# Second gate/up: the last product's sum behind the split of the third quarter's rest, and both FFNs' row factor behind the down product

## The chip, the core and the metric

The kernel runs on one core of a Trainium2 chip. The metric is the device time of one execution in microseconds; lower is better.

## What is computed

One encoder layer on x of 256 rows and 2048 columns, all in float32, with F = 5632:

```python
def rms_norm(x, gain):
    return x * rsqrt(mean(x * x, axis=-1) + EPS) * gain

def swiglu(h, w_gate, w_up, w_down):
    return (silu(h @ w_gate) * (h @ w_up)) @ w_down

x = x + 0.5 * swiglu(rms_norm(x, ffn1_norm), ffn1_w_gate, ffn1_w_up, ffn1_w_down)
x = x + concat(rms_norm(s5(u)), rms_norm(attention(q, k, v))) @ w_out    # [u|q|k|v] = rms_norm(x) @ w_in
x = x + 0.5 * swiglu(rms_norm(x, ffn2_norm), ffn2_w_gate, ffn2_w_up, ffn2_w_down)
x = x + rms_norm((p @ w_ple_proj) * sigmoid(rms_norm(x) @ w_ple_gate))
```

The factor rsqrt(...) of rms_norm is one number for each row. A product of rms_norm(x) with weights is therefore computed as the product of (x times gain) with them, and the row factor r is multiplied in later.

## The kernel before

**Tiles.** T = 256 rows make two row tiles of 128 (TT = 2). F is cut into 11 column blocks of 512 (NF = 11, NB = 512), and the contraction over 2048 into four quarters of four 128-row pieces. Weights arrive by SP's DMAs as `raw` tiles, from a pool with five buffers.

**Precision.** A float32 operand is split into a high and a low part. `split` does so for two 128-row pieces at once (a half of a quarter, 128x1024): a CAST on ACT (L181) makes the high part, and a subtraction on DVE (L184) the low one. A half of a quarter and one row tile then take six matmuls on PE: high by high, low by high and high by low, twice. The results of splits lie in two rings, `whi`/`wlo` and `shi`/`slo`, which `weight_pair` hands out in turn.

**The FFNs.** In FFN1 most blocks go through the class `Seven`, which computes a 2 by 2 block product by seven products of sums. FFN2's gate and up use `Wide` for blocks f = 1 to 10. In blocks f = 1 to 9 half of the third quarter goes into the seven products too (`narrow`, the flag `n`), and the other half of that quarter, its rest, is added as an ordinary product: for the gate's columns as the first work of `column(0)`, for the up columns as the first of `column(1)`.

**`Wide.seven`.** Its products gather in the banks b2, b3, b4, b5 and b8. b3 and b8 lie in one `aux` tile, the others are `acc` tiles. The last product but one ends in b4. Then follow, in the code of before: `add(t, b21)`, two DVE additions of 128x1024 (L721) that make the operand of the last product, called "11"; `handed(b8, b4)`, an ACT copy with its sign turned (L704); the split of both sides' rests; the first half of the gate's column; the split of the sum; and product "11", which is added to b4. b4 takes no new matmul before `handed` has read it.

**The order of the work.** The program is written in one order, and a scheduler sets each engine's queue from it ahead of the run. Some instructions are kept in program order (`pin`), and `tc.issue_after` makes an instruction follow another. Each engine works through its own queue in order and waits for the others by semaphores.

**The row factor.** The norm object `xn` holds r as a tile with one column for each row tile; `xn.rs(t)` is its column t. It is used as the scale of the gate's silu (L860, L890, L925) and as the scalar of the last multiplication, up times r times gate (L870 in FFN2's `Wide` blocks, L910 in FFN1's `Seven` blocks, L950 in the others). Behind the down product `gather` (L967) adds 0.5 times a bank into x, 40 times in the two FFNs.

Of the kernel before, what the change touches and what calls it, by code (L numbers as in the profile page):

```python
# [9 lines left out]
F32 = mybir.dt.float32  # L10
# [3 lines left out]
ALU = mybir.AluOpType  # L14
AX = mybir.AxisListType

P = 128
# [9 lines left out]
NB = 512  # L27
# [6 lines left out]
def layer_kernel(ctx: ExitStack, tc: tile.TileContext, a: dict, shapes: dict, out: bass.AP):  # L34
    nc = tc.nc
# [8 lines left out]
    TT = T // P  # L44
# [7 lines left out]
    cpool = ctx.enter_context(tc.tile_pool(name="const", bufs=1))  # L52
# [46 lines left out]
    def step():  # L99
        for g in list(beside):  # L100
            if next(g, beside) is beside:
                beside.remove(g)
# [38 lines left out]
    def place_x():  # L141
        for t in range(TT):
            x = wp.tile([P, ND, NB], F32, tag="raw", name=uid("x"), bufs=5)
            xt[t][:] = [x[:, n, :] for n in range(ND)]
# [5 lines left out]
                nc.gpsimd.dma_start(xt[t][n], rows[t * P : (t + 1) * P, n * NB : (n + 1) * NB])  # L150

    place_x()
    scr_x = dramp.tile([T, D], F32, name="scr_x")

    def load_x(n):
# [482 lines left out]
    class Wide:  # L638
# [67 lines left out]
        def seven(self):  # L706

            if ring[0] is None:
                ring[:] = [self.turns, 0]
            n = self.narrow is not None  # L710
            b11 = self.load(0, 0)
            if n:
                gn, un = self.load_both(0)
                tn = self.narrow[1].tile([P, 2, NB], F32, tag="sumn", name=uid("sumn"))
            b12 = self.load(1, 0)
            b22, b21 = self.load(1, 1), self.load(0, 1)
            t = [self.pool.tile([P, 2, NB], F32, tag="sum", name=uid("sum"), bufs=2) for _ in range(2)]

            def add(x, y):
                for o, u, v in zip(t, x, y):  # L720
                    nc.vector.tensor_tensor(out=o, in0=u, in1=v, op=ALU.add)  # L721

            def add_one(o, x, y):
                nc.vector.tensor_tensor(out=tn[:, o], in0=x, in1=y, op=ALU.add)

            b2, b5 = acc(), acc()
            p = self.prepare(b11)
            self.product(b2, self.left("00"), p, True, not n)
            if n:
                pg, = self.prepare([gn])  # L730
                self.one(b2, "00", pg, 0)
            step()
            add(b11, b12)
            for u, v in zip(b12, b22):
                nc.gpsimd.dma_start(u, v, accum_op=ALU.add)
            if n:
                add_one(0, gn[:, 0], un[:, 0])
                nc.gpsimd.dma_start(un[:, 0], un[:, 1], accum_op=ALU.add)
                add_one(1, tn[:, 0], un[:, 1])
            p = self.prepare(t)  # L740
            double = aux()
            b3, b8 = double[:, :NB], double[:, NB:]
            self.handed(b3, b2)
            self.product(b5, self.left(0), p, True, not n)
            if n:
                self.one(b2, "10", pg, 1)
                pt, = self.prepare([tn])
                self.one(b5, 0, pt, 0)
            step()
            add(t, b22)  # L750
            p = self.prepare(t)
            self.product(b3, self.left(1), p)
            if n:
                self.one(b3, 1, pt, 1)
                add_one(0, tn[:, 1], gn[:, 1])
            step()
            p = self.prepare(b21)
            self.product(b2, self.left("10"), p)
            step()
            b4 = acc()  # L760
            p = self.prepare(b22)
            self.handed(b4, b3)
            self.product(b3, self.left(3), p)
            step()
            p = self.prepare(b12)
            self.product(b4, self.left(2), p)
            if n:
                pu, = self.prepare([un])
                self.one(b4, 2, pu, 0)
                self.one(b3, 3, pu, 1)  # L770
            step()
            add(t, b21)
            self.handed(b8, b4)
            self.banks = ((b2, b4), (b3, b8))
            self.double, self.five = double, b5
            self.rest = [[], []]
            if n:
                self.rest = [[(self.act(2), (1, *list(weight_split(u, 2))[0][1:]), False)] for u in self.load_both(1)]
            self.first = self.halves_of(0)
            self.half(0, *next(self.first))  # L780
            p = self.prepare(t)
            self.product(b4, self.left("11"), p)
            if n:
                pt, = self.prepare([tn[:, :1]])
                self.one(b4, "11", pt, 0)
            step()

        def halves_of(self, side):

            w, n0 = self.ws[side]  # L790
            yield from self.rest[side]
            for kb in (3,) if self.narrow else (2, 3):
                part = self.act(kb)
                for half in list(weight_halves(w, 4 * kb, 4, n0)):
                    yield part, half, kb == 3 and half[0] == 1
# [11 lines left out]
    def ffn(i, xn, nxt, bg=None):  # L807
# [30 lines left out]
        for f in range(NF):  # L838
# [9 lines left out]
            if not bg and f:  # L848
                joined = f in range(1, NF - 1)
                s = Wide(  # L850
                    xn, sums, ((wg, f * NB), (wu, f * NB)), sevens, turns, (third, narrow) if joined else None
                )
                s.seven()
                sg, hh, five = com("sg"), com("h"), com("sq")
                put_off(0, nc.scalar.copy, five, s.five)
                s.column(0)

                def gate(s=s, sg=sg):
                    for t in range(TT):
                        nc.scalar.activation(sg[:, t * NB : (t + 1) * NB], s.banks[0][t], AF.Silu, scale=xn.rs(t))  # L860

                put_off(0, gate)
                s.column(1)
                nc.vector.tensor_tensor(
                    out=hh.rearrange("p (t n) -> p t n", t=TT), in0=s.double.rearrange("p (t n) -> p t n", t=TT),
                    in1=five.unsqueeze(1).to_broadcast([P, TT, NB]), op=ALU.add,
                )
                for t in range(TT):
                    cols = slice(t * NB, (t + 1) * NB)
                    nc.vector.scalar_tensor_tensor(  # L870
                        out=hh[:, cols], in0=hh[:, cols], scalar=xn.rs(t), in1=sg[:, cols], op0=ALU.mult, op1=ALU.mult
                    )
                if f == NF - 2:
                    side.close()
                    hp = pools.enter_context(phase(f"h{i}b"))
                put_off(2, turned, hp, f, hh)
                continue
            if bg and (f >= early or f in alone):
# [25 lines left out]
                    put_off(0, opened, s)  # L904
                put_off(0, gated, s)

                def ended(s, g=gate_cols, u=up_cols, hh=hh, f=f, hp=hp):
                    nc.vector.tensor_tensor(out=hh, in0=s.banks[3.8], in1=hh, op=ALU.add)
                    for t in range(TT):
                        nc.vector.scalar_tensor_tensor(  # L910
                            out=u[t], in0=u[t], scalar=xn.rs(t), in1=g[t], op0=ALU.mult, op1=ALU.mult
                        )
                    put_off(2, turned, hp, f, hh)

                s.column(1, (1, 2, 3) if f in alone else (2, 3), True)
# [31 lines left out]
                start(prep)  # L947
            hh = com("h")
            for t in range(TT):
                nc.vector.scalar_tensor_tensor(  # L950
                    out=hh[:, t * NB : (t + 1) * NB], in0=pu[t], scalar=xn.rs(t),
                    in1=sg[:, t * NB : (t + 1) * NB], op0=ALU.mult, op1=ALU.mult,
                )
            put_off(2, turned, hp, f, hh)

        fetch_x(a["x"][0] if bg else scr_x)
# [6 lines left out]
            split(in_32(hi), in_32(lo), rows(k))  # L963
            return hi, lo

        def gather(x, ps, scale):
            nc.vector.scalar_tensor_tensor(out=x, in0=ps, scalar=scale, in1=x, op0=ALU.mult, op1=ALU.add)  # L967

        def opened(s, n):
            sg = com("sg")  # L970
            one, six = sg[:, :NB], sg[:, NB:]
            nc.scalar.copy(one, s.bank(1))
            nc.vector.tensor_tensor(out=six, in0=s.bank(6), in1=one, op=ALU.add)
            gather(xt[0][n], one, 0.5)
            for t in range(TT):
                gather(xt[t][n + 1], s.bank(5), 0.5)
            gather(xt[0][n + 1], six, -0.5)
            nc.vector.tensor_tensor(out=one, in0=s.bank(7), in1=six, op=ALU.add)
            gather(xt[1][n], one, 0.5)
            gather(xt[1][n + 1], one, -0.5)  # L980

        plans = (
            (("c", 3), ("c", 4), ("s", 0), ("c", 5), ("c", 6), ("s", 1), ("c", 7), ("c", 8), ("s", 2), ("c", 9), ("c", 10)),
# [18 lines left out]
        for n in range(0, ND, 2):  # L1002

            def end(side):
                m = n + side
                for t, z in enumerate(((2, 4), (3, 8))[side]):
                    gather(xt[t][m], s.bank(z), 0.5)
                put_off(0 if m == ND - 2 or m == ND - 1 and m < nxt.early else 2, nxt.block, m)

            s = Seven(kept, summed, ((wd, n * NB), (wd, (n + 1) * NB)), sevens, turns)  # L1010
# [1018 lines left out]
```

## Time and profile before

| what | value |
| --- | --- |
| median of 3 runs (lowest to highest) | 1821.94 us (1821.84 to 1822.03) |
| the profiled execution's own time | 1821.02 us |
| its span, first to last instruction | 1819.2 us |
| mean granted TensorE clock | 0.999 |

Time between the span and the execution's own time lies around the span. The engines are called PE (TensorE's matmuls), PEld (its weight loads), DVE (VectorE), ACT (ScalarE), POOL (GpSimd) and SP (SyncE, whose queue issues DMAs). In the timeline a row is start, duration, engine, line, operation, what it writes and reads, and in brackets how long the engine had been idle and what ended that. In a list of waits, a row is who waited for whom: total us, times, longest.

### The profile page before, as it was taken

How to read it: one execution, taken by the hardware profiler on the slowest of the kernel's cores; microseconds unless marked ns; L12 is line 12 of the kernel's file. 1: busy time of each engine (PE TensorE's matmuls, PEld its weight loads, DVE VectorE, ACT ScalarE, POOL GpSimd, SP SyncE). 2: the span in 40 equal slices, each digit the busy share in tenths (PEclk: the TensorE clock that was granted, in tenths of full speed). 3: DMA queues.
4: the chain of work that ended last, by engine and by line, in shares of the span. 5: the costliest groups of instructions: out<-in, count | busy, mean ns of one | idle time of the engine just before them, and what ended most of it. 6: DMA issues, size and time to landing. Idle time of an engine off the chain costs nothing.

```text
span 1819.2 us, 24321 instructions
## 1 busy us (share of the span) xinstructions
PE 1804.9 (99%) x8897; PEld 1491.7 (82%) x8897; DVE 1560.5 (86%) x1824; ACT 1094.0 (60%) x1285; POOL 166.1 (9%) x266
## 2 busy tenths in 40 slices
PE   9999999999999999999999999999999999999998
PEld 7888888888888888888898888788878788888887
DVE  8978889999998896697567889999999988889775
ACT  7445455656565665456695566666667656566564
POOL 0020100000000001110021002020202230000000
PEclk9999999999999999999999999999999999999999
DMA  8799867687776667674646678888877776666563
GB/s 320 268 293 300 264 224 232 233 260 228 261 262 224 187 227 250 203 252 161 218 144 223 215 267 258 278 263 253 252 229 237 256 255 240 223 206 229 192 244 127
DMA packets 106792, 430.25 MB, mean 236 GB/s; under 512 B 24784, under 2 KB 42608, under 8 KB 66576
## 3 DMA queue, kind: packets, MB, share of 16 engines
q1 hardware_dynamic: 91168, 384.28, 59.9%
q0 software_dynamic: 14784, 43.01, 10.8%
q8 instruction: 69, 1.13, 0.3%
q10 hardware_dynamic: 720, 1.41, 0.2%
q14 instruction: 51, 0.42, 0.1%
HBM read 372.41 MB, written 10.88 MB: 211 GB/s over the span
## 4 chain that ended last, share of the span: by engine, by line
PE 93%; DVE 3%; issue 1%; ACT 1%; SPq 1%; DMA 1%; DVEq 0%; ACTq 0%
PE acc L325 16%; PE acc L328 15%; PE acc L334 15%; PE aux L325 7%; PE aux L334 7%; PE aux L328 7%; PE acc L687 3%; PE acc L691 3%; PE acc L695 3%; PE acc L512 2%; PE acc L515 2%; PE acc L513 2%; PE aux L515 2%; PE aux L512 2%; PE aux L513 2%
## 5 line engine op out<-in xcount | busy, mean ns | idle before, releaser
L184 DVE TENSOR_TENSOR wlo<-raw,whi 128x1024 fp32r<-128x1024 f32 x484 | 585.9, 1224 | 128.8 <-ACT whi L181 128.2
L181 ACT CAST whi<-raw 128x1024 fp32r<-128x1024 f32 x484 | 503.4, 1050 | 316.0 <-PE acc L328 188.4
L325 PE MATMUL acc<-whi,nhi 128*128 128x512 f32 x884 | 347.4, 393 | 5.0 <-ACT whi L277 2.5
L328 PE MATMUL acc<-whi,nlo 128*128 128x512 f32 x884 | 344.4, 390 | 0.0
L334 PE MATMUL acc<-wlo,nhi 128*128 128x512 f32 x884 | 245.0, 389 | 0.0
L184 DVE TENSOR_TENSOR slo<-raw,shi 128x1024 fp32r<-128x1024 f32 x182 | 221.4, 1218 | 15.9 <-ACT shi L181 15.5
L181 ACT CAST shi<-raw 128x1024 fp32r<-128x1024 f32 x182 | 190.3, 1049 | 68.8 <-PE acc L328 21.5
L325 PEld LDWEIGHTS acc<-whi,nhi 128*128 128x128 f32 x884 | 165.9, 188 | 43.4 <-ACT whi L277 3.5
L334 PEld LDWEIGHTS acc<-wlo,nhi 128*128 128x128 f32 x884 | 165.8, 188 | 34.8 <-DVE wlo L184 0.2
L328 PEld LDWEIGHTS acc<-whi,nlo 128*128 128x128 f32 x884 | 166.0, 188 | 33.5 <-DVE nlo L278 0.2
L181 ACT CAST whi<-sum 128x1024 fp32r<-128x1024 f32 x81 | 85.2, 1053 | 123.4 <-DVE sum L519 63.2
L184 DVE TENSOR_TENSOR wlo<-sum,whi 128x1024 fp32r<-128x1024 f32 x81 | 98.4, 1220 | 8.0 <-ACT whi L181 7.9
L181 ACT CAST shi<-sum 128x1024 fp32r<-128x1024 f32 x54 | 56.8, 1052 | 77.3 <-DVE sum L519 46.3
L325 PE MATMUL aux<-whi,nhi 128*128 128x512 f32 x216 | 84.0, 389 | 0.0
L328 PE MATMUL aux<-whi,nlo 128*128 128x512 f32 x216 | 84.0, 389 | 0.0
L580 POOL DMA_DIRECT2D raw<-raw x23 | 20.1, 875 | 602.3 <-DVE sum L519 355.3
L325 PE MATMUL aux<-whi,hhi 128*128 128x512 f32 x176 | 68.5, 389 | 0.0
L328 PE MATMUL aux<-whi,hlo 128*128 128x512 f32 x176 | 68.5, 389 | 0.0
L184 DVE TENSOR_TENSOR slo<-sum,shi 128x1024 fp32r<-128x1024 f32 x54 | 65.9, 1220 | 2.8 <-ACT shi L181 2.6
L334 PE MATMUL aux<-wlo,nhi 128*128 128x512 f32 x216 | 65.2, 389 | 0.0
L519 DVE TENSOR_TENSOR sum<-sum,raw 128x1024 f32<-128x1024 f32 x50 | 61.1, 1222 | 0.8
L230 POOL DMA_DIRECT2D hT<-mid x96 | 51.6, 553 | 97.2 <-DVE mid L217 36.6
(477 smaller groups left out, 3580.9 us busy)
## 6 DMA issues: line engine op xcount, KB each, us to landing
raw<-in_ffn_w_down SPq DMA_DIRECT2D x88, 1024.0 KB, 4.9
raw<-in_ffn_w_up SPq DMA_DIRECT2D x79, 1024.0 KB, 7.2
raw<-in_ffn_w_gate SPq DMA_DIRECT2D x77, 1024.0 KB, 6.8
raw<-in_w_in SPq DMA_DIRECT2D x32, 1024.0 KB, 5.3
raw<-raw POOLq DMA_DIRECT2D x45, 512.0 KB, 7.7
raw<-in_w_out SPq DMA_DIRECT2D x16, 1024.0 KB, 5.1
raw<-in_w_ple_gate SPq DMA_DIRECT2D x16, 1024.0 KB, 5.1
raw<-in_ffn_w_gate SPq DMA_DIRECT2D x21, 512.0 KB, 7.5
```

The costliest lines, as they stand in the source:

```text
L181: copy = nc.scalar.copy(hi, src)
L184: rest = nc.vector.tensor_tensor(out=lo, in0=src, in1=hi.bitcast(F32), op=ALU.subtract)
L325: nc.tensor.matmul(ps[t], lhsT=lh, rhs=hi[:, j, cols], start=start and j == 0, stop=False, skip_group_check=joined)
L328: nc.tensor.matmul(ps[t], lhsT=ll, rhs=hi[:, j, cols], start=False, stop=False, skip_group_check=joined)
L334: nc.tensor.matmul(ps[t], lhsT=lh, rhs=lo[:, j, cols], start=False, stop=stop and j == 1, skip_group_check=joined)
L512: nc.tensor.matmul(ps, lhsT=lh[j], rhs=hi[:, j], start=begin and j == 0, stop=False)
L513: nc.tensor.matmul(ps, lhsT=ll[j], rhs=hi[:, j], start=False, stop=False)
L515: nc.tensor.matmul(ps, lhsT=lh[j], rhs=lo[:, j], start=False, stop=z in final and j == 1)
L519: nc.vector.tensor_tensor(out=t, in0=x, in1=y, op=ALU.add)
L687: nc.tensor.matmul(ps, lhsT=lh[n * i + j], rhs=hi[:, j], start=fresh and i == 0 and j == 0, stop=False, skip_group_check=True,)
L691: nc.tensor.matmul(ps, lhsT=ll[n * i + j], rhs=hi[:, j], start=False, stop=False, skip_group_check=True)
L695: nc.tensor.matmul(ps, lhsT=lh[n * i + j], rhs=lo[:, j], start=False, stop=last and i == len(parts) - 1 and j == n - 1, skip_group_check=True,
```

## The change

Two edits, made together.

1. In `Wide.seven`, for blocks with `narrow`, the split of the gate's rest is written ahead of the last product's sum. `add(t, b21)` is forced behind the DVE instruction of that split (`self.last`), and it now stands behind the fetch of the first half of the gate's column. The up side's rest is split after product "11" in place of ahead of it. `rest_of` is new.
2. In both FFNs, h is no longer multiplied by r. The two DVE instructions per block, 128x512 with a row scalar each, become one multiplication of 128x1024 by the gate (at L950 two of 128x512). `gather` multiplies by r instead: a small tile `by_row` holds 0.5 r and -0.5 r, made by two small DVE instructions ahead of each down product, and `gather` reads its scalar from there in place of the constant 0.5 or -0.5. The gate's silu keeps its r.

```diff
+    by_row = cpool.tile([P, 2 * TT], F32, name="by_row")
...
             step()
-            add(t, b21)
             self.handed(b8, b4)
...
-            self.rest = [[], []]
+            self.rest = []
             if n:
-                self.rest = [[(self.act(2), (1, *list(weight_split(u, 2))[0][1:]), False)] for u in self.load_both(1)]
+                raws = self.load_both(1)
+                self.rest.append(self.rest_of(raws[0]))
             self.first = self.halves_of(0)
-            self.half(0, *next(self.first))
+            half = next(self.first)
+            with tc.issue_after(self.last) if n else ExitStack():
+                add(t, b21)
+            self.half(0, *half)
             p = self.prepare(t)
             self.product(b4, self.left("11"), p)
             if n:
                 pt, = self.prepare([tn[:, :1]])
                 self.one(b4, "11", pt, 0)
+                self.rest.append(self.rest_of(raws[1]))
             step()

+        def rest_of(self, raw):
+            hi, lo = weight_pair()
+            self.last = split(hi, lo, raw)[1]
+            return self.act(2), (1, hi, lo), False
...
-                for t in range(TT):
-                    cols = slice(t * NB, (t + 1) * NB)
-                    nc.vector.scalar_tensor_tensor(
-                        out=hh[:, cols], in0=hh[:, cols], scalar=xn.rs(t), in1=sg[:, cols], op0=ALU.mult, op1=ALU.mult
-                    )
+                nc.vector.tensor_tensor(out=hh, in0=hh, in1=sg, op=ALU.mult)
...
-        def gather(x, ps, scale):
-            nc.vector.scalar_tensor_tensor(out=x, in0=ps, scalar=scale, in1=x, op0=ALU.mult, op1=ALU.add)
+        for sign in range(2):
+            nc.vector.tensor_scalar(
+                by_row[:, TT * sign : TT * sign + TT], xn.r[:, :TT], 0.5 - sign, None, op0=ALU.mult
+            )
+
+        def gather(t, n, ps, sign=0):
+            nc.vector.scalar_tensor_tensor(
+                out=xt[t][n], in0=ps, scalar=by_row[:, TT * sign + t : TT * sign + t + 1], in1=xt[t][n],
+                op0=ALU.mult, op1=ALU.add,
+            )
```

The line numbers of the changed kernel are higher by one up to the first edit (L181 is L182 there, L704 is L705, L721 is L722), and by more behind it. Tiles carry numbers that differ between the two kernels.

ACT's queue in block f = 3 before, from the earlier `handed` (b3 to b4) to the one that copies b4 to b8. raw_10281 is the piece with both rests, sum_10107 and sum_10108 are the halves of the last sum, sumn_10100 is the narrow block's sum, and raw_10334 the next weights:

```order
L704 ACTIVATE acc_10226<-aux_10153 128x512
L181 CAST whi_10284<-raw_10281 128x1024
L181 CAST shi_10288<-raw_10281 128x1024
L181 CAST whi_10304<-sum_10107 128x1024
L181 CAST whi_10324<-sumn_10100 128x512
L181 CAST shi_10308<-sum_10108 128x1024
L181 CAST shi_10336<-raw_10334 128x1024
L181 CAST whi_10340<-raw_10334 128x1024
L704 ACTIVATE aux_10153<-acc_10226 128x512
```

And with the change, without that first row (raw_10273 has the rests, raw_10328 the next weights):

```order
L182 CAST whi_10276<-raw_10273 128x1024
L182 CAST shi_10294<-sum_10101 128x1024
L182 CAST shi_10314<-sumn_10094 128x512
L182 CAST whi_10298<-sum_10102 128x1024
L182 CAST whi_10321<-raw_10273 128x1024
L705 ACTIVATE aux_10147<-acc_10220 128x512
L182 CAST shi_10330<-raw_10328 128x1024
L182 CAST whi_10334<-raw_10328 128x1024
```

The CAST of the up side's rest has gone from ahead of the sums' casts to behind them, and `handed` stands ahead of the next weights' two casts and still behind the sums'. DVE's queue at the same place before, from the last sum on:

```order
L721 TENSOR_TENSOR sum_10107<-sum_10107,raw_10105 128x1024
L721 TENSOR_TENSOR sum_10108<-sum_10108,raw_10105 128x1024
L184 TENSOR_TENSOR wlo_10285<-raw_10281,whi_10284 128x1024
L184 TENSOR_TENSOR slo_10289<-raw_10281,shi_10288 128x1024
L184 TENSOR_TENSOR wlo_10305<-sum_10107,whi_10304 128x1024
L184 TENSOR_TENSOR slo_10309<-sum_10108,shi_10308 128x1024
L184 TENSOR_TENSOR wlo_10325<-sumn_10100,whi_10324 128x512
```

And with the change, from the low part of the gate's rest on:

```order
L185 TENSOR_TENSOR wlo_10277<-raw_10273,whi_10276 128x1024
L722 TENSOR_TENSOR sum_10101<-sum_10101,raw_10099 128x1024
L722 TENSOR_TENSOR sum_10102<-sum_10102,raw_10099 128x1024
L185 TENSOR_TENSOR slo_10295<-sum_10101,shi_10294 128x1024
L185 TENSOR_TENSOR slo_10315<-sumn_10094,shi_10314 128x512
L185 TENSOR_TENSOR wlo_10299<-sum_10102,whi_10298 128x1024
L185 TENSOR_TENSOR wlo_10322<-raw_10273,whi_10321 128x1024
```

The low part of the gate's rest (wlo_10285 before, wlo_10277 now) has moved ahead of the two sums, and that of the up side's rest (slo_10289 before, wlo_10322 now) behind the sums' low parts.

More of the change, by code (lines that the diff above doesn't have):

```diff
@@ L785, in seven @@
                 self.one(b4, "11", pt, 0)
+                self.rest.append(self.rest_of(raws[1]))
             step()
+        def rest_of(self, raw):
+            hi, lo = weight_pair()
+            self.last = split(hi, lo, raw)[1]
+            return self.act(2), (1, hi, lo), False
         def halves_of(self, side):
             w, n0 = self.ws[side]
-            yield from self.rest[side]
+            if self.rest:
+                yield self.rest[side]
             for kb in (3,) if self.narrow else (2, 3):
@@ L905, in ffn, with ended @@
                 put_off(0, gated, s)
-                def ended(s, g=gate_cols, u=up_cols, hh=hh, f=f, hp=hp):
+                def ended(s, sg=sg, hh=hh, f=f, hp=hp):
                     nc.vector.tensor_tensor(out=hh, in0=s.banks[3.8], in1=hh, op=ALU.add)
[L909 to L912, printed above, removed]
+                    nc.vector.tensor_tensor(out=hh, in0=hh, in1=sg, op=ALU.mult)
                     put_off(2, turned, hp, f, hh)
@@ L949, in ffn @@
             for t in range(TT):
[L950 to L953, printed above, removed]
+                cols = slice(t * NB, (t + 1) * NB)
+                nc.vector.tensor_tensor(out=hh[:, cols], in0=pu[t], in1=sg[:, cols], op=ALU.mult)
             put_off(2, turned, hp, f, hh)
@@ L973, in opened @@
             nc.vector.tensor_tensor(out=six, in0=s.bank(6), in1=one, op=ALU.add)
-            gather(xt[0][n], one, 0.5)
+            gather(0, n, one)
             for t in range(TT):
-                gather(xt[t][n + 1], s.bank(5), 0.5)
-            gather(xt[0][n + 1], six, -0.5)
+                gather(t, n + 1, s.bank(5))
+            gather(0, n + 1, six, 1)
             nc.vector.tensor_tensor(out=one, in0=s.bank(7), in1=six, op=ALU.add)
-            gather(xt[1][n], one, 0.5)
-            gather(xt[1][n + 1], one, -0.5)
+            gather(1, n, one)
+            gather(1, n + 1, one, 1)
         plans = (
@@ L1006, in end @@
                 for t, z in enumerate(((2, 4), (3, 8))[side]):
-                    gather(xt[t][m], s.bank(z), 0.5)
+                    gather(t, m, s.bank(z))
                 put_off(0 if m == ND - 2 or m == ND - 1 and m < nxt.early else 2, nxt.block, m)
```

## The prediction

> **What bounds the kernel now.** I read the page first for the engines' shares, then the busy time by stage, then what PE waits for in the stage that the first edit touches, and then that stage's queues step by step. The page:
>
> ```profile
> span 1819.2 us, 24321 instructions
> ...
> PE 1804.9 (99%) x8897; PEld 1491.7 (82%) x8897; DVE 1560.5 (86%) x1824; ACT 1094.0 (60%) x1285; POOL 166.1 (9%) x266
> ...
> PE 93%; DVE 3%; issue 1%; ACT 1%; SPq 1%; DMA 1%; DVEq 0%; ACTq 0%
> ```
>
> PE runs 1804.9 of 1819.2 us and makes 93% of the chain that ended last. The change leaves the matmuls as they are, so no more than the 14.3 us in which PE is idle can be gained, and what can be lost is new idle time of PE. By stage (the second gate/up runs from about 1060 to 1460 us, the second down product from there to 1700):
>
> ```profile
> core 0: us, PE busy (x) PEld busy (x) DVE busy (x) ACT busy (x) POOL busy (x), PEclk, DMA share, GB/s
> 1076.00:1117.00 41.00, 41.00 (x181) 33.71 (x180) 41.00 (x41) 28.55 (x33) 2.61 (x3) 1.00 0.72 236
> ...
> 1158.00:1199.00 41.00, 39.56 (x173) 32.16 (x173) 40.42 (x41) 27.28 (x31) 2.63 (x3) 1.00 0.75 240
> ...
> 1321.00:1362.00 41.00, 39.52 (x174) 32.18 (x173) 40.93 (x41) 26.23 (x30) 2.63 (x3) 1.00 0.74 237
> ...
> 1403.00:1443.00 40.00, 38.96 (x171) 31.70 (x170) 38.52 (x37) 25.89 (x29) 1.71 (x2) 1.00 0.70 238
> ```
>
> ```profile
> 1100.00:1460.00 360.00, 356.04 (x1561) 291.97 (x1560) 347.11 (x336) 239.07 (x265) 68.08 (x111) 1.00 0.80 251
> 1460.00:1700.00 240.00, 240.00 (x1060) 198.75 (x1059) 208.21 (x211) 144.18 (x157) 16.01 (x26) 1.00 0.67 229
> ```
>
> The granted clock is 1.00 in each. In the second gate/up, DVE is nearly full: 347.11 of 360 us, and 41.00 of 41.00 in the block that begins at 1076. PE lacks 360 − 356.04 = 4.0 us there, all of it in the three blocks shown (1.44, 1.48 and 1.04). In the down product PE lacks nothing and DVE has 31.8 us free. PE's own waits in the gate/up stretch:
>
> ```profile
> PE acc L325 <- ACT aux L704: 2.8, 3, 0.9
> PE acc L325 <- ACT shi L181: 1.1, 2, 0.5
> ```
>
> Three times PE waits for `handed` (L704, the copy of b4 to b8 with its sign turned), and twice for a CAST. Both stand in ACT's queue behind the splits that the change reorders. Block 3 (f = 3), ACT's queue first, then DVE's, then PE's:
>
> ```profile
> 1171.55 1.05 ACT L181 CAST whi<-sum 128x1024 fp32r<-128x1024 f32 x1 [4.52 <-DVE sum L721]
> 1172.50 0.62 ACT L181 CAST whi<-sumn 128x512 fp32r<-128x512 f32 x1
> 1173.02 1.05 ACT L181 CAST shi<-sum 128x1024 fp32r<-128x1024 f32 x1
> 1173.98 1.03 ACT L181 CAST shi<-raw 128x1024 fp32r<-128x1024 f32 x1
> 1174.92 1.04 ACT L181 CAST whi<-raw 128x1024 fp32r<-128x1024 f32 x1
> 1175.87 0.57 ACT L704 ACTIVATE aux<-acc 128x512 f32<-128x512 f32 x1
> ```
>
> ```profile
> 1170.24 2.35 DVE L721 TENSOR_TENSOR sum<-sum,raw 128x1024 f32<-128x1024 f32 x2
> 1172.51 1.22 DVE L184 TENSOR_TENSOR wlo<-raw,whi 128x1024 fp32r<-128x1024 f32 x1
> 1173.64 1.22 DVE L184 TENSOR_TENSOR slo<-raw,shi 128x1024 fp32r<-128x1024 f32 x1
> ```
>
> ```profile
> 1173.93 0.62 PE L334 MATMUL acc<-wlo,nhi 128*128 128x512 f32 x2
> 1175.07 0.50 PE L325 MATMUL acc<-shi,nhi 128*128 128x512 f32 x1 [0.51 <-ACT shi L181]
> 1176.49 0.51 PE L325 MATMUL acc<-whi,nhi 128*128 128x512 f32 x1 [0.93 <-ACT aux L704]
> ```
>
> DVE makes the last sum (two L721 of 1.22 us) at 1170.24. ACT idles 4.52 us until the first half is there, then casts it, the narrow sum, the second half and two pieces of raw weights back to back, and only then gets to `handed` at 1175.87. PE, out of work at about 1174.4, resumes 0.05 us after its end. So the path here is: first sum on DVE, five CASTs on ACT, `handed`, PE.
>
> **The first edit: the last sum behind the split of the gate's rest.** What it removes is the up side's rest split ahead of the sum's own splits. What it puts ahead of the sum is one L184, the gate's rest (forced by the new dependence). Back to back, DVE instructions of this size start 1.13 us apart (1172.51 to 1173.64), so the sum begins 1.13 us later. Nothing on ACT makes up for that, as the new order keeps `handed` behind the sum's casts. Worked through for block 3, with DVE's queue as it stood: first sum at 1170.24 + 1.13 = 1171.37, done 1.22 later at 1172.59; its CAST 0.09 behind (as 1171.55 stands to 1171.46), at 1172.68; the narrow sum's CAST 0.95 later at 1173.63; the second sum's CAST 0.52 later at 1174.15; the CAST of the up side's rest at 1175.10; `handed` at 1176.05, done 1176.63; PE at 1176.68 in place of 1176.49. PE also loses the one matmul that filled 0.23 us of that wait (the hoisted half's first, now behind). Block 3: 0.19 + 0.23 = **+0.42 us**.
>
> The other blocks go the same way, with their own casts ahead of `handed`. I worked blocks 5, 7 and 9:
>
> ```profile
> 1250.68 2.35 DVE L721 TENSOR_TENSOR sum<-sum,raw 128x1024 f32<-128x1024 f32 x2
> ...
> 1333.12 2.35 DVE L721 TENSOR_TENSOR sum<-sum,raw 128x1024 f32<-128x1024 f32 x2
> ...
> 1415.04 2.35 DVE L721 TENSOR_TENSOR sum<-sum,raw 128x1024 f32<-128x1024 f32 x2
> ```
>
> ```profile
> 1256.51 0.58 ACT L704 ACTIVATE aux<-acc 128x512 f32<-128x512 f32 x1
> ...
> 1338.93 0.57 ACT L704 ACTIVATE aux<-acc 128x512 f32<-128x512 f32 x1
> ...
> 1420.85 0.58 ACT L704 ACTIVATE aux<-acc 128x512 f32<-128x512 f32 x1
> ```
>
> ```profile
> 1256.81 0.84 PE L325 MATMUL acc<-whi,nhi 128*128 128x512 f32 x2
> ...
> 1339.56 0.50 PE L325 MATMUL acc<-shi,nhi 128*128 128x512 f32 x1 [0.93 <-ACT aux L704]
> ...
> 1421.48 0.50 PE L325 MATMUL acc<-whi,nhi 128*128 128x512 f32 x1 [0.94 <-ACT aux L704]
> ```
>
> In each the first sum's CAST starts 1.13 + 1.22 + 0.09 = 2.44 us behind the time shown for the sum. Block 5: CAST at 1253.12, then (0.95, 0.52, 0.95, 0.95, 0.95: sum, narrow sum, second sum, rest, next raw) `handed` at 1257.44, where it was 1256.51: **+0.93**, and PE feels all of it, since it had been free at 1257.04 and `handed` was already the last to come, at 1257.09. Block 9 has the same five casts in another order: 1417.48 + 4.32 = 1421.80 against 1420.85, **+0.95**. Block 7 has the narrow sum cast ahead of the first sum, then first sum at 1335.56, the second at 1336.69 (it waits for DVE: 1333.12 + 1.13 + 2.35 + 0.09), the rest at 1337.64 and two more raw pieces: `handed` at 1340.49 against 1338.93, **+1.56**. Blocks 4 and 6 are built like block 5, but for one raw piece fewer or more ahead of `handed`; I take 0.6 each, between 0 and its 0.93. In blocks 1, 2, 8 and 10, `handed` comes no later by the same count, and I take nothing. Sum: 0.42 + 0.93 + 0.95 + 1.56 + 1.2 = **+5.1 us**.
>
> **The second edit: the row factor.** Prices from these groups:
>
> ```profile
> L870 DVE SCALAR_TENSOR_TENSOR h<-h,sm,sg x20: 743/746/749, 1115.3 to 1484.0; 128x512 f32<-128x512 f32 x20
> ...
> L721 DVE TENSOR_TENSOR sum<-sum,raw x40: 1215/1220/1227, 1075.3 to 1451.8; 128x1024 f32<-128x1024 f32 x40
> ...
> L910 DVE SCALAR_TENSOR_TENSOR h<-h,sm,sg x14: 743/746/750, 185.7 to 484.3; 128x512 f32<-128x512 f32 x14
> ...
> L967 DVE SCALAR_TENSOR_TENSOR x<-sg,x x16: 683/684/687, 567.1 to 1674.9; 128x512 f32<-128x512 f32 x16
> ```
>
> In the second gate/up, two L870 (2 × 0.746 = 1.49 us) become one multiply of the size and kind of L721 (1.22): −0.27 us of DVE in each block. [...]
>
> DVE is full in these blocks, so I let the relief of 0.27 reach the last sum once in each of the six blocks that pay: 6 × 0.27 = **−1.6 us**. At the first FFN's L910 (7 pairs) and L950 the same relief meets a PE that does not wait there: nothing. Behind the down products the 40 gathers now read a row factor: 0.746 − 0.684 = 0.062 us each, 2.5 us of DVE over two stages; the one shown has 31.8 us free, so I book nothing (2.5 if that cover fails). The two tiny scalings ahead of each down product have no row like them; the nearest, a gather, puts them under 0.7 us each, in DVE's free time: nothing.
>
> **What is late next.** The raw pieces that had been cast ahead of `handed`, and the up side's rest, are now split up to one slot (1.13 us) later, and PE needs them next. If PE's wait at `handed` covers that, it costs 0; if each of the seven blocks 3 to 9 pays a slot again, 7 × 1.13 = 7.9 us. I take one slot, **+1.1**, as PE is then late itself. Total: 5.1 − 1.6 + 1.1 = **+4.6 us**. The profiled execution took 1821.0 us (span 1819.2, 1.8 around it), 0.9 below the median of 1821.9; on the median this makes **1826.5 us**.
>
> **The rivals.** A measurement of this kernel can tell about 0.2%, 3.6 us, from no change: 1818.3 to 1825.6.
>
> *DVE is the bound and is relieved (faster).* DVE has more busy time than PE's weight load, and PE's lost 4.0 us lie where DVE is fullest. If 0.27 a block adds up from block to block (1.6 us by the sixth), it outweighs the 1.13 of the moved split from the fifth block on; if the gate's rest, split earlier, also ends the waits for the two CASTs, all 4.0 us go: 1817.9. Against it: the windows of 1158 and 1403 show 0.6 and 1.5 us of DVE free, so lateness does not add up, and the moved split comes at once. 0.14. [...] The PE rows above speak against it, since ACT's queue order releases PE.
>
> *Nothing comes of it (no change).* The sum's lateness and DVE's relief cancel, if raw weights and buffers let DVE run ahead in the even blocks too: 5.1 − 10 × 0.27 = 2.4, 1824.3, or less where ACT's 34% of free time absorbs it. For it: blocks 1, 2, 8 and 10 pay nothing. With the case that only the gathers are exposed (+2.5, 1824.4) 0.28.
>
> *Slower, the forecast.* The split's slot decides wherever `handed` is already the last to come, from a sum later by over 0.05 us in block 5. With the knock-on at its full size it is 5.1 − 1.6 + 7.9 = 11.4, 1833.3. 0.58.
>
> **The numbers.** 1826.5 us. The likeliest case's own range is 1825.6 to 1833.5; the whole range reaches down to the full gain, 1817.5, since 42 in 100 lie below the forecast's own case. Faster 0.14, same 0.28, slower 0.58.
>
> **What would show it.** In the trace after: the sum at L722 stands one L185 later; PE's waits for `handed` grow from 2.8 us to 6 or more and from three blocks to six; the waits for a CAST of the rest vanish; PE's busy share of 1100 to 1460 falls below 356 us of 360. DVE's multiply by the gate is one instruction of 1.22 us in a block, and a gather takes about 0.746. I am wrong if `handed` comes no later, if those waits shrink, or if PE's time is lost in the down product or at casts behind `handed` and not at it.

## The result and the profile after

The changed kernel takes 1825.4 us (median of 12 runs, 1823.6 to 1828.0) against 1821.7 us (12 runs, 1821.0 to 1822.8) in the same sessions; the ratio is 1.0023, with an interval of 1.0015 to 1.0031. It is slower, by about 4 us, and its runs lie further apart. Measured once more, in a later session, it took 1825.2 us against 1820.7 us (1.0026, 1.0017 to 1.0036).

The profiled execution of the changed kernel is the slowest of the 12: 1827.95 us, with a span of 1826.1 us, 6.9 us over that of before. The page and the busy time by stage:

```profile
PE 1809.2 (99%) x8897; PEld 1496.3 (82%) x8897; DVE 1560.4 (85%) x1811; ACT 1091.1 (60%) x1285; POOL 164.9 (9%) x266
```

```profile
1158.00:1199.00 41.00, 38.08 (x160) 30.70 (x159) 39.74 (x39) 25.59 (x30) 2.63 (x3) 0.96 0.77 246
1321.00:1362.00 41.00, 37.99 (x160) 30.73 (x159) 38.82 (x38) 25.95 (x30) 2.61 (x3) 0.96 0.72 239
1403.00:1443.00 40.00, 37.21 (x164) 30.47 (x163) 38.33 (x37) 25.27 (x29) 1.71 (x2) 1.00 0.74 243
1100.00:1460.00 360.00, 351.04 (x1528) 288.52 (x1527) 340.17 (x321) 231.77 (x260) 63.05 (x101) 0.99 0.78 245
```

In the second gate/up PE is now idle for 9.0 of 360 us, where it was 4.0. The three windows with idle time are the same as before, each with more of it. Two of them have a granted clock of 0.96 where it was 1.00: PE is not only idle longer there, it also runs slower for a while. Its waits there:

```profile
PE acc L326 <- ACT aux L705: 6.0, 4, 2.8
PE acc L326 <- ACT shi L182: 2.1, 1, 2.1
PE acc L688 <- ACT aux L705: 0.9, 1, 0.9
```

The waits for `handed` (L705) have gone from 2.8 to 6.0 us, with one more of 0.9 us for the block's earlier `handed`, the one from b2 to b3 that L688 waits for. Block 3, on ACT:

```profile
1173.27 1.05 ACT L182 CAST shi<-sum 128x1024 fp32r<-128x1024 f32 x1 [6.41 <-DVE sum L722]
1174.23 0.61 ACT L182 CAST shi<-sumn 128x512 fp32r<-128x512 f32 x1
1174.74 1.04 ACT L182 CAST whi<-sum 128x1024 fp32r<-128x1024 f32 x1
1175.69 1.04 ACT L182 CAST whi<-raw 128x1024 fp32r<-128x1024 f32 x1
1176.64 0.57 ACT L705 ACTIVATE aux<-acc 128x512 f32<-128x512 f32 x1
```

ACT idles for 6.41 us before the sum's first CAST (4.52 before the change), then has four casts ahead of `handed`. The CAST of the up side's rest, which used to fit into that idle time, is the last of them. PE, at the same place:

```profile
1174.60 0.61 PE L335 MATMUL acc<-wlo,nhi 128*128 128x512 f32 x2
1177.26 0.50 PE L326 MATMUL acc<-whi,nhi 128*128 128x512 f32 x1 [2.05 <-ACT aux L705]
1177.60 0.58 PE L329 MATMUL acc<-whi,nlo 128*128 128x512 f32 x1
1177.98 0.63 PE L326 MATMUL acc<-whi,nhi 128*128 128x512 f32 x1
1178.40 0.63 PE L329 MATMUL acc<-whi,nlo 128*128 128x512 f32 x1
1178.83 1.06 PE L335 MATMUL acc<-wlo,nhi 128*128 128x512 f32 x2
1179.68 0.63 PE L688 MATMUL acc<-shi,hhi 128*128 128x512 f32 x1
```

PE waits 2.05 us and then its matmuls start 0.43 us apart in place of 0.23, until 1181.1. The same happens at 1345.0 to 1348.3, behind block 7's wait, and not behind block 9's, though that one is the longest (2.8 us). Each of the two slow stretches costs 1.6 us: eight or so matmul starts that are 0.20 us late.

The second edit did what it says, as two groups of DVE's lines show:

```profile
L879 DVE TENSOR_TENSOR h<-h,sg x10: 1218/1220/1230, 1115.3 to 1490.4; 128x1024 f32<-128x1024 f32 x10
...
L974 DVE SCALAR_TENSOR_TENSOR x<-sg,by_row,x x16: 746/747/751, 566.7 to 1682.9; 128x512 f32<-128x512 f32 x16
```

One multiplication of 1.22 us in a block, and gathers of 0.747 us in place of 0.684. In the window of the second down product (1465 to 1705 in this trace) PE is busy for 240.00 of 240 us, so the gathers cost nothing there.

### The profile page after: what moved, and what is told of

It reads as the page before. It is cut to its first block, busy times and chain, and to the rows that moved or that the text cites. A ratio compares the mean times of both kernels' runs of the same rounds, so it can differ in the third digit from the quotient of the medians.

```text
span 1826.1 us, 24283 instructions
## 1 busy us (share of the span) xinstructions
PE 1809.2 (99%) x8897; PEld 1496.3 (82%) x8897; DVE 1560.4 (85%) x1811; ACT 1091.1 (60%) x1285; POOL 164.9 (9%) x266
## 5 line engine op out<-in xcount | busy, mean ns | idle before, releaser
L182 ACT CAST whi<-raw 128x1024 fp32r<-128x1024 f32 x483 | 502.3, 1050 | 309.8 <-PE acc L329 178.3
L182 ACT CAST shi<-raw 128x1024 fp32r<-128x1024 f32 x183 | 191.4, 1049 | 69.5 <-DMA raw<-in_ffn_w_down 19.0
L182 ACT CAST whi<-sum 128x1024 fp32r<-128x1024 f32 x80 | 84.2, 1052 | 126.3 <-DVE sum L520 63.2
L182 ACT CAST shi<-sum 128x1024 fp32r<-128x1024 f32 x55 | 57.8, 1052 | 93.9 <-DVE sum L520 45.5
```

The source lines that it names most:

```text
L182: copy = nc.scalar.copy(hi, src)
```

## The experiments

Times are medians against the kernel before on the same chip (its medians lay between 1820.7 and 1821.9 us); the ratio's interval is at 95%.

**The first edit alone.** All of `Wide.seven`'s changes, without those to the row factor. 

> Only the first edit (the last sum behind the split of the gate's rest, the up side's rest later); the row factor stays where it was. Theory A (the sum's casts stand ahead of handed on ACT, and the sum is one split later on DVE): without the relief on DVE at least what the whole change cost, +4 to +7 us, with PE's long waits for handed in blocks 3, 7 and 9. Theory B (the cost comes from the second edit, the gathers that read a row factor): +0 to +1.5 us.

Measured: 1822.2 us, ratio 1.0005 (0.9997 to 1.0014). It is not +4 to +7 us, and by its number it looks like theory B. The trace says otherwise: the waits for `handed` are there, but shorter.

```profile
PE acc L325 <- ACT aux L704: 4.9, 4, 1.5
PE acc L325 <- ACT shi L181: 0.2, 1, 0.2
```

The scheduler has set ACT's queue a little differently here. In block 3 only the sum's own three casts stand ahead of `handed`, which starts 3.75 us behind the sum; with both edits it is four casts and 4.71 us. In block 7 it is four casts against five. None of its waits in this view is over 1.5 us, and none in the trace is followed by slow matmuls (the granted clock is 1.00 between 1100 and 1460 us). Two of its 11 runs took 1825.5 and 1825.7 us, at a mean clock of 0.997; the other nine took 1820.8 to 1822.9 us, at 0.998 to 1.000.

**The second edit alone.** The row factor behind the down product, and the old order in `Wide.seven`. 

> Only the second edit (the row factor behind the down product); the order of the sum and the rests is that of before. Theory A: DVE is relieved by 0.27 us a block and nothing else moves, so -2 to +0.5 us, and PE's waits for handed in blocks 3, 7 and 9 are no longer than before (2.8 us in all). Theory B: +2 to +4 us, with PE idle in a down product.

Measured: 1821.3 us, ratio 0.9997 (0.9989 to 1.0006): no change. The waits for `handed` are 3.0 us in all, as before (2.8). The gathers cost nothing that can be measured, which excludes theory B: the interval ends at +1.1 us, and PE is busy for 240.00 of 240 us in the second down product. Of DVE's relief little reaches PE: between 1100 and 1460 us it is busy for 356.24 us in this trace, where it was 356.04. In block 3 the sum starts at 1169.00 in place of 1170.24, but `handed` only 0.75 us earlier, at 1175.12 in place of 1175.87, with five casts between them on ACT as before.

**The whole change, with the sum at its old place.**

```diff
             step()
+            add(t, b21)
             self.handed(b8, b4)
...
             half = next(self.first)
-            with tc.issue_after(self.last) if n else ExitStack():
-                add(t, b21)
             self.half(0, *half)
```

> The whole change, but the last sum stands at its old place, ahead of handed and not forced behind the split of the gate's rest; the up side's rest is still split late. Theory A, with the forced place of the sum as the cause: the 1.13 us of the split go from ahead of the sum, and with them 3 to 5 us: -2 to +1.5 us against before. Theory C (what costs is that the up side's rest and the next weights are split later): +3 to +5 us as in the whole change.

Measured: 1823.3 us, ratio 1.0011 (1.0002 to 1.0019). It lies between the theories: some of the loss seems to go with the sum's place, but not all, and the interval overlaps the change's own. In block 3 `handed` is as late as in the change (1176.56 against 1176.64), though the sum starts 2.0 us earlier, as six casts stand ahead of it:

```profile
1171.29 1.05 ACT L182 CAST shi<-sum 128x1024 fp32r<-128x1024 f32 x1 [5.26 <-DVE sum L722]
1172.25 0.61 ACT L182 CAST shi<-sumn 128x512 fp32r<-128x512 f32 x1
1172.77 1.05 ACT L182 CAST whi<-sum 128x1024 fp32r<-128x1024 f32 x1
1173.72 1.04 ACT L182 CAST whi<-raw 128x1024 fp32r<-128x1024 f32 x1
1174.67 1.04 ACT L182 CAST shi<-raw 128x1024 fp32r<-128x1024 f32 x1
1175.61 1.04 ACT L182 CAST whi<-raw 128x1024 fp32r<-128x1024 f32 x1
1176.56 0.57 ACT L705 ACTIVATE aux<-acc 128x512 f32<-128x512 f32 x1
```

The up side's rest and two pieces of the next weights stand between the sum's casts and `handed`. ACT is idle for 5.26 us ahead of the sum's casts; the kernel before has cast the rest by then. So it is not the sum's place on DVE alone: what is cast ahead of `handed`, and when, decides.

**The whole change, with `handed` first.** The sum's casts are issued behind `handed` on ACT; nothing else is touched, and the sum is still forced behind the split of the gate's rest.

```diff
-            nc.scalar.activation(out, ps, AF.Copy, scale=-1.0)
+            return nc.scalar.activation(out, ps, AF.Copy, scale=-1.0).ins
...
-            self.handed(b8, b4)
+            taken = self.handed(b8, b4)
...
-            p = self.prepare(t)
+            with tc.issue_after(taken):
+                p = self.prepare(t)
```

> The whole change, and the CASTs of the last sum are issued behind handed on ACT, so that handed no longer waits for the sum. Theory A: PE's waits for handed all but go (under 0.5 us in all between 1060 and 1465 us), and the time falls to or below that of before: -4 to 0 us. Theory C: +3 to +5 us as in the whole change, the wait only moves from handed to a CAST.

Measured: 1816.1 us, ratio 0.997 (0.9958 to 0.9981), faster than both kernels, by more than expected. Block 3 on ACT:

```profile
1172.91 0.58 ACT L705 ACTIVATE aux<-acc 128x512 f32<-128x512 f32 x1 [4.84 <-PE aux L696]
1173.40 1.04 ACT L182 CAST shi<-sum 128x1024 fp32r<-128x1024 f32 x1
1174.35 1.05 ACT L182 CAST whi<-sum 128x1024 fp32r<-128x1024 f32 x1
```

`handed` is now released by PE itself, and PE is busy for the whole of 1100 to 1460 us:

```profile
1100.00:1460.00 360.00, 360.00 (x1584) 296.27 (x1583) 348.75 (x331) 239.87 (x271) 70.48 (x114) 1.00 0.81 254
```

DVE does more in this window than in the change's (348.75 against 340.17 us), because more of the program fits into it. A full DVE did not bound these blocks. Theory C falls: no wait for a CAST takes the place of the one for `handed`.

**The kernel before, with `handed` first.** The same edit on the kernel before. 

> The kernel before with one edit: the last sum's CASTs behind handed on ACT. The sum stays ahead of the rest's split and the row factor stays in h. Theory A (handed's place in ACT's queue makes the waits, the sum's place on DVE does not count by itself): the waits for handed go, 3 to 6 us faster than before. Theory D (the moved sum is needed as well, since otherwise the product of the sum waits for its split): at most 2 us faster, with new waits of PE for a split of the sum.

Measured: 1815.5 us, ratio 0.997 (0.9958 to 0.9982). The one edit gains 5.3 us, and neither part of the change is needed for it. The same window:

```profile
1100.00:1460.00 360.00, 359.67 (x1582) 296.20 (x1581) 351.27 (x340) 239.44 (x270) 70.28 (x114) 1.00 0.81 254
```

**The second edit, with `handed` first.** 

> The second edit and handed first, without the first edit. Theory A: 3 to 6 us faster than before, within 1 us of the run with both edits and handed first. Theory D: at most 2 us faster.

Measured: 1815.6 us, ratio 0.9969 (0.9956 to 0.9981). The three versions with `handed` first lie within 0.7 us of one another, so the change's two edits are worth nothing that can be measured once the wait is gone, nor do they cost anything.

**The change again.** 

> The changed kernel once more, on the same chip as the others. +3 to +5 us against before. If slow matmuls (0.427 us apart in place of 0.227) behind the long waits are part of it, they show again behind waits of over 2 us, in some of blocks 3, 7 and 9, and 1.6 to 1.8 us each; if the two places of the first trace were chance, none.

Measured: 1825.2 us (1823.1 to 1828.3), ratio 1.0026. In this trace, of a run at the low end (1821.3 us of span), no matmul of the second gate/up is slow (the granted clock is 1.00 between 1100 and 1460 us), though the waits are there again:

```profile
PE acc L326 <- ACT aux L705: 5.0, 3, 2.0
PE acc L326 <- ACT shi L182: 1.4, 1, 1.4
PE acc L688 <- ACT aux L705: 0.5, 1, 0.5
```

Block 3's wait lasts 2.03 us here against 2.05 us in the first trace, where slow matmuls followed. So they don't depend on the length of the wait alone. Of the two outcomes that were expected, this trace has the one for chance; the next two runs show what the chance is. The mean clock of the nine runs goes with their times: the fastest, at 1823.06 us, has 0.999, and the slowest, at 1828.30 us, has 0.995.

**Idle times of known length.** The kernel with both edits and `handed` first, in which `handed` is repeated in some blocks, so that PE waits longer.

```diff
-            taken = self.handed(b8, b4)
+            for _ in range(1 + (0, 3, 5, 6, 7, 8, 9, 11, 14, 0)[self.ws[0][1] // NB - 1]):
+                taken = self.handed(b8, b4)
```

> The change with handed first, and handed repeated in blocks 2 to 9 (3, 5, 6, 7, 8, 9, 11 and 14 times more), so that PE idles longer from block to block. One more costs ACT 0.51 us, PE's cover is about 0.9 us: idle times of about 0.6, 1.7, 2.2, 2.7, 3.2, 3.7, 4.7 and 6.2 us. If the length of the idle time alone decides on the slow matmuls, there is one threshold and all longer ones are followed by them; if it also matters when it falls, some of 2 to 3.5 us are and some are not.

Measured: waits of 1.3 us (no slow matmuls) and of 2.5 to 8.1 us (seven, each followed by slow ones). The slow matmuls end at 1182.60, 1226.97, 1274.77, 1319.14, 1366.92, 1414.71 and 1465.90 us, worked out from the starts of the matmuls. The steps between these are 44.37, 47.80, 44.37, 47.78, 47.79 and 51.19 us: 13, 14, 13, 14, 14 and 15 times 3.413. The shortest of them, around 1178:

```profile
1178.23 0.50 PE L326 MATMUL acc<-whi,nhi 128*128 128x512 f32 x1 [2.38 <-ACT aux L705]
1178.57 0.39 PE L329 MATMUL acc<-whi,nlo 128*128 128x512 f32 x1
1178.80 0.39 PE L326 MATMUL acc<-whi,nhi 128*128 128x512 f32 x1
1179.03 0.50 PE L329 MATMUL acc<-whi,nlo 128*128 128x512 f32 x1
1179.33 1.05 PE L335 MATMUL acc<-wlo,nhi 128*128 128x512 f32 x2
```

PE ran at full speed (starts 0.23 us apart) for 0.9 us behind the wait and only then slowed down (0.43 us apart): the clock changed here at a point of the grid, 3.4 us ahead of the end at 1182.60, and not when the wait ended.

**The same, with the longest first.** The repeats are 14, 11, 9, 8, 7, 6, 5 and 3, in blocks 1 to 8. 

> As the dose run, with the longest waits first: handed repeated 14, 11, 9, 8, 7, 6, 5 and 3 times more in blocks 1 to 8, so idle times of about 8, 6, 4.5, 4, 3.7, 3.1, 2.5 and 1.3 us. If the clock is set by whole stretches of 3.41 us on a fixed grid, by how much of a stretch PE was idle, all slow stretches end a whole number of 3.41 us apart, every idle time of over 4 us is followed by them, 1.3 us is not, and those of 2.5 to 3.1 us are or are not by where they fall. If the length alone counts, the ends lie anywhere.

Measured: six waits of 3.2 to 8.1 us, all followed by slow matmuls, and one of 1.3 us that is not. The repeats meant for about 2.5 us, in block 7, gave two waits of 0.5 and 0.6 us, which says nothing on that length. The slow stretches end 14.0, 14.0, 14.0, 13.0 and 14.0 times 3.413 us apart.

**The sum's casts only ahead of `handed`.** The whole change, in which the casts of the up side's rest and of the next weights are also issued behind `handed`; the sum and its casts stay where the change has them.

```diff
+                with tc.issue_after(taken):
-                self.rest.append(self.rest_of(raws[1]))
+                    self.rest.append(self.rest_of(raws[1]))
...
-                for half in list(weight_halves(w, 4 * kb, 4, n0)):
+                with tc.issue_after(self.taken):
+                    both = list(weight_halves(w, 4 * kb, 4, n0))
+                for half in both:
```

> The whole change, with the CASTs of the up side's rest and of the next weights issued behind handed on ACT; the sums' own casts (three in blocks 3 to 9) stay ahead of it, and the sum stays behind the split of the gate's rest. If handed's place is a matter of how many casts of 0.95 us stand ahead of it, its waits fall by one cast in block 3 (2.2 to 1.2 us) and by two in blocks 7 and 9, no wait is over 2 us, no slow matmuls follow, and the time is 1 to 4 us below that of before. If what counts is that the sum itself is late, the waits stay and the time is 3 to 5 us above.

Measured: 1819.3 us, ratio 0.9989 (0.998 to 0.9998): 2.6 us below before, and 6 us below the change, with the sum as late on DVE as in it. `handed` starts 3.8 us behind the sum in block 3 (4.7 in the change), PE's wait there is 1.3 us (2.2), and the waits of blocks 5, 7 and 9 are gone (the waits of block 3 by the starts of the matmuls). So each cast that stands ahead of `handed` counts, as expected. What is left in this trace:

```profile
PE acc L326 <- ACT whi L182: 1.6, 1, 1.6
PE acc L326 <- ACT aux L705: 1.1, 1, 1.1
PE acc L688 <- ACT aux L705: 0.9, 1, 0.9
```

The 1.1 us are block 3's `handed`, and the 0.9 us its earlier `handed`. The 1.6 us, in block 10, come with this run's own edit: ACT is idle for 7.58 us there until `handed` starts at 1452.30, and the cast that PE waits for may only follow it.

## Why the prediction was right, and where it was not

The total was right: +4.6 us forecast, about +4 measured, with the forecast's sign, and the loss lies on the path that was forecast, from the sum over ACT's casts and `handed` to PE. Several terms of the sum were not right, and that the total came so close is in part luck: the blocks paid less than booked, most of the relief didn't come, and a slower clock, which the sum doesn't have, made up for a part (3.2 us in the first trace). "The split's slot decides" is also only half of it: with the sum as late, and only the sums' casts ahead of `handed`, the kernel is 2.6 us faster than before. By block, the time that PE lost at the second `handed` and just ahead of it, from the starts of the matmuls (the distance of two neighbouring starts less the usual 0.23 us):

| block | before | the change | the change again | first edit alone | predicted for the change, beyond before |
| --- | --- | --- | --- | --- | --- |
| 3 | 1.88 | 2.21 | 2.19 | 1.46 | +0.42 |
| 5 | 0.11 | 0.40 | 0.06 | 1.21 | +0.93 |
| 7 | 1.91 | 3.44 | 2.73 | 1.24 | +1.56 |
| 9 | 1.47 | 2.95 | 2.16 | 1.67 | +0.95 |
| 4 and 6 | 0.04 | 0.00 | 0.00 | 0.35 | +1.2 |
| 3, the earlier `handed` | 0.00 | 1.03 | 0.61 | 0.00 | (one slot of 1.1, elsewhere) |

*The path on ACT.* It was right to the tenth. From the sum's start on DVE to `handed`, the prediction had 4.68 us in block 3, 5.63 in block 5, 6.24 in block 7 and 5.63 in block 9; the trace of the change has 4.71, 5.67, 6.24 and 5.65. Counting casts of 0.95 us in the new order was enough.

*Blocks 4, 5 and 6.* "Blocks 4 and 6 are built like block 5 ... I take 0.6 each" failed: they paid nothing, and block 5 paid 0.29 us of its 0.93, or nothing in the second trace. The likely reason, which no run isolates, is that PE has waited in block 3 and so comes later to those blocks; the prediction priced each block as if PE arrived at its old distance. The sum over the blocks, 5.1 us, was 3.6 us in the first trace, and 1.7 in the second (by the table's rows, without the last).

*DVE's relief.* "I let the relief of 0.27 reach the last sum once in each of the six blocks that pay: −1.6" was not borne out. With the second edit alone the kernel gained 0.4 us, nothing measurable (0.9997; the interval, −2.0 to +1.1 us, doesn't exclude 1.6), and in the trace PE's busy time rose by only 0.2 us in the 360 of the window. The rival that DVE bounds these blocks falls by another run: in the kernel before with `handed` first, a change of ACT's order alone, PE is busy for 359.67 us of its window, with DVE busier than before (351.27 against 347.11 us).

*What is late next.* One slot was booked for split weights behind `handed`. A loss of that size came (1.03 and 0.61 us), at another place: the earlier `handed` of block 3, behind a sum that DVE could begin only when its raw weights had landed.

```profile
1146.23 2.36 DVE L722 TENSOR_TENSOR sum<-raw,raw 128x1024 f32<-128x1024 f32 x2 [2.85 <-DMA raw<-in_ffn_w_up]
```

In the trace of before this pair starts at 1146.08, only 0.15 us earlier, and the wait of PE isn't there. The new order of DVE's queue makes most of the difference. Before, the narrow block's first sum (L724, L725 now) stood ahead of the pair, in the wait for the weights; now it stands behind it. Before, then after, with the sum that comes next:

```profile
1145.34 0.68 DVE L724 TENSOR_TENSOR sumn<-raw 128x512 f32<-128x512 f32 x1
1152.37 1.22 DVE L721 TENSOR_TENSOR sum<-sum,raw 128x1024 f32<-128x1024 f32 x1
```

```profile
1149.65 0.68 DVE L725 TENSOR_TENSOR sumn<-raw 128x512 f32<-128x512 f32 x1
1153.12 1.22 DVE L722 TENSOR_TENSOR sum<-sum,raw 128x1024 f32<-128x1024 f32 x1
```

That sum starts 0.75 us later, and the earlier `handed`, behind its cast, 0.76 us later (1158.62 against 1157.86). PE comes there 0.5 us earlier than before, by the starts of the same matmuls. No run moves the narrow sum alone.

*The slow clock was missing.* Behind two of the waits of 2 us and more in the first trace, those of blocks 3 and 7, PE ran at half its clock (granted 0.50) for 3.4 us. That cost 2 × 1.6 = 3.2 us. By the starts of the same matmuls in the traces of before and after, the changed kernel is 0.3 us ahead at 1060 us and 7.05 us behind at the end of the second gate/up, so it loses 7.3 us there, and all of the 6.9 by which the span rose comes from this stage. The waits of the table add up to 4.6 us more than before, the slow clock to 3.2, and the remaining −0.5 us is in smaller gaps. In the second trace, without slow stretches in this stage, the change costs 2.1 us of span. Whether the clock makes the rest in the median is argued from the mean clocks of the runs alone: of the changed kernel's 21 runs, the seven with a mean clock of 0.999 took 1823.1 to 1825.4 us, and the nine with 0.997 or less 1825.2 to 1828.3 us. The mean counts slow stretches of other stages too, and nineteen of these runs have no trace.

This is also why the two edits don't add up, with +0.4 and −0.4 us alone, and about +4 together. The trace of the first edit alone has waits of at most 1.7 us, by the table. With the second edit, the scheduler's new order puts one more cast ahead of `handed` in blocks 3 and 7, and the waits grow past 2 us; behind two of them the clock fell to 0.50 in the first trace. The order and the waits are shown; that the clock is the rest of the difference in the median is argued from the runs' clocks.

*The rivals.* That nothing comes of it had about the right sum, +2.4 us, for a run without slow stretches, but by luck: its reason, DVE's relief in ten blocks, hardly reached PE. The signs named ahead held for PE's busy share (351.0 of 360), for the waits' sum and for the two DVE durations. They failed for the number of blocks, which is four and not six, and for the CASTs, one of which PE still waits for in block 7 (2.1 us). The prediction took the CASTs that PE waits for to be those of the rest. In block 3 of before, by ACT's queue, the first cast behind the sums' and the one that PE waited for is that of the next weights (raw_10334).

## What to carry to other kernels

Look at which instruction the waiting engine is released by, and then at what stands ahead of it in its own engine's queue: a copy of 0.58 us that frees a bank stood behind 2 to 5 us of casts whose operands came late, and issuing it first was worth 5.3 us, more than any other order tried here. Price a chain of such waits with the first one's delay carried to the next, and reckon with more than their length: here a wait of 2.05 us on TensorE cost 1.6 us more in one run, and one of 2.03 us nothing more in another.

## What the runs showed of the hardware

TensorE's granted clock fell to 0.50 behind some waits. Four traces have slow matmuls in the second gate/up: the first of the change, the one with the sum at its old place (a granted clock of 0.99 between 1100 and 1460 us, where the first edit alone has 1.00) and the two with repeats. In the first of the change and in those with repeats, matmuls of 512 columns started 0.427 us apart in place of 0.227 while the granted clock was 0.50. Two such stretches of the first run with repeats:

```profile
1179.20:1182.60 3.40, 3.40 (x9) 2.62 (x9) 3.40 (x4) 3.40 (x5) 0.00 (x0) 0.50 0.54 212
1223.60:1226.90 3.30, 3.30 (x9) 2.55 (x8) 2.70 (x3) 3.30 (x5) 0.00 (x0) 0.50 0.96 385
```

The ends lie on a grid of 3.413 us in these three traces (in the first one of the change, 1181.07 and 1348.33 us, 49.0 steps; in the other two, the steps given with the runs). Laid on that grid, the waits of the second gate/up agree in them and in the second trace of the change: from the full clock, the stretches in which PE idled for 1.96 us or more were followed by a slow one, and those with up to 1.86 us were not. Block 7's loss in the first trace, 3.4 us in two waits, has 1.45 us in one stretch and 1.96 in the next, and the third is slow (granted clock 0.50); block 9's 2.95 us is cut by the grid into 1.31 and 1.63 us, and nothing follows. The second trace of the change has its grid from a slow stretch near the program's start:

```profile
8.72:12.12 3.40, 3.33 (x8) 2.65 (x9) 2.38 (x6) 2.35 (x7) 0.00 (x0) 0.50 1.03 414
```

Carried on from there in steps of 3.413 us, which is an estimate, this grid cuts block 3's loss of 2.19 us into 1.27 and 0.92 us, and block 7's of 2.73 us into 1.86 and 0.87 us, and nothing follows either. The grid lay differently in the two traces of the change, and so a wait of 2.05 us cost 1.6 us more in one and a wait of 2.03 us nothing more in the other.
